# Five modulation vectors summed along the row on VectorE, with the weights' columns on the partitions

## The chip, the cores and the metric

One core of one Trainium2 chip. The metric is device microseconds of one execution of the whole program, the median of three runs. Engines are named as the profile names them: PE is TensorE's matrix multiply, PEld its weight load, DVE is VectorE, ACT ScalarE, POOL GpSimd, and SP the engine whose queue issues nearly all loads.

## The reference, cut to what matters

Two blocks of two residual layers each work on 256 tokens of 1024 features. Each layer takes three vectors of 1024 numbers (shift, scale, gate) from a condition vector `c`:

```
sc = jax.nn.silu(c)
shift, scale, gate = jnp.split(sc @ mod_w[l] + mod_b[l], 3, axis=-1)
hx = modulate(rmsnorm(x, norm_g[l]), shift[:, None], scale[:, None])
...
x = x + gate[:, None] * out_x
```

Block 2 does the same with its own condition `c_2`, six vectors from one weight of 1024 by 6144. Where a second sequence (a context) is modulated too, the same weight is also multiplied by a second condition. The large matrix products between are what most of the time goes to.

## The kernel before, in words

Features lie on the 128 partitions, eight tiles of them, and tokens along the free dimension. Weights come from memory in pieces of 1 MB (128 partitions by 2048), all into one pool of ten slots (`w_p`). A main weight piece is split into a high and a low part (`split`, lines 308 to 310: a cast on ACT at L309 and a subtraction on DVE at L310, in stretches of 512), and every product runs as three products of the parts (`mm3`, L357 to L359).

The modulation weights come through the same pool, 40 chunks of 1 MB after the first eight (`mod_groups`, loads at L502), placed by hand between the main pieces: the lists `L0`, `L1`, `L2`, `L2B` and `L3` give the order of the work in layer 0, layer 1, the mixers of block 2, their output products and the feed-forward, and `md` or `ml` in them means the next chunk. A framework then orders the instructions of each engine by priority, which follows the program's order unless something is put ahead of it, and adds the waits. An instruction with nothing to wait for can be issued far ahead of its place.

Vectors that the context needs too (and three others) are made on TensorE (L515). Five vectors, named in `ON_DVE` at line 85 (`gate1`, `gate2`, `shift3`, `scale3`, `gate3`), are needed for x alone and are made by `x_vector` (lines 468 to 486). A chunk holds two tiles of 128 input features on the partitions, with the 1024 output columns along the row. DVE multiplies each row by its feature's condition value and adds it to a running `part` of 128 by 1024: L476 for the first tile, L478 for the seven others. What is then left is the sum over the 128 partitions, and eight products of `part` with a column of ones on TensorE do that (L482), into a PSUM bank, from which DVE adds the bias (L484). `part` sits in one of the eleven slots of the pool `t4` from the first chunk to the last.

Places that the text speaks of: the end of layer 0, where the steps `ga` and `ra` of `L0` finish and three chunks of `gate1` lie; `residual` (L617 on), which adds the gated output to `X` (L625); and the products begun on an X that is not normed yet (`cols_early`, L606) while the norm is still being computed.

Of the kernel before, what the change touches and what calls it, by code (L numbers as in the profile page):

```python
# [37 lines left out]
# Layer 0 after its first four pieces: weight pieces in order, with modulation chunks (md) between them; the  # L38
# convolution fills what they leave.
# [15 lines left out]
# Layer 1 likewise: (step, group, half).  # L55
# [7 lines left out]
# The mixers of block 2 likewise.  # L63
# [11 lines left out]
# The feed-forward: pairs of up projections, each pair's down projection one piece later.  # L75
# [11 lines left out]
P = 128  # L87
# [48 lines left out]
def pack(inp):  # L136
# [56 lines left out]
    for name, m in L3:  # L193
        if name == "up":
            wp.append(piece_k8(up[:, 128 * m:128 * (m + 1)], up[:, F + 128 * m:F + 128 * (m + 1)]))
        elif name == "down":
# [6 lines left out]
                      for k in range(8)]).reshape(8, KT, P, 256).transpose(0, 2, 1, 3)  # L203
# [3 lines left out]
    mp = np.concatenate([first.reshape(8, P, 2048), full(blk(m0, 2), blk(m1, 0)), half(blk(m1, 1)), half(blk(m1, 2)),  # L207
                         *(half(blk(mw2, i)) for i in range(6))])

    # the convolution's taps in fours, [feature of 32, tap of four] by [feature tile, four, group of 32]  # L210
# [9 lines left out]
           "cst": constants()}  # L220
# [3 lines left out]
def build(tc, gates, wp, mp, vec, xT, cT, c2T, tok, cst, out, dbg=None):  # L224
# [60 lines left out]
    def order_after(i, before):  # L285
        """Keeps two instructions of one engine in order."""
        tc.add_manual_dep(i, before.name, mybir.DependencyInfo(mybir.DependencyClass.NoSync, mybir.DependencyReason.DATA),
                          reason="engine order")

    def act(out, in_, func, **kw):  # L290
        """An activation that needs a table set: kept in order with the others that do."""
        i = nc.scalar.activation(out, in_, func, **kw).ins
        if "last" in tables:
            order_after(i, tables["last"])
        tables["last"] = i
        return i

    def table(name):
        """The table set of the activations that follow."""
# [15 lines left out]
    def halves(raw, width):  # L315
        """A weight piece's parts."""
# [27 lines left out]
    def piece(last=False):  # L344
        """The next weight piece; the ones after it are on their way (fewer behind the last of a layer)."""
# [15 lines left out]
    def mm_w(o, w, x, at, start, stop):  # L361
        """o += w[at].T @ x, in float32 (w and x whole) or in three float32r products of their parts."""
# [5 lines left out]
    def mm_cols(o, w, j, h):  # L368
        """o[128 columns, tokens] over all of D."""
# [3 lines left out]
    def cols2(pc, h):  # L373
        """Two column tiles in one bank."""
# [6 lines left out]
    def toks(o, w, h, s):  # L381
        """o[128 tokens, 256 columns] over all of D."""
# [6 lines left out]
    def mm_rows(banks, pc, x, first, last):  # L389
        """Adds two K tiles (x(k): parts) to all of the 1024 output columns."""  # L390
# [13 lines left out]
    def spread(col):  # L404
        """[128 tokens, 2] -> a bank's [128, 256], the same in all partitions."""
# [8 lines left out]
    def rstd_of(ms, n, eps):  # L414
        """(sum / n + eps) ** -0.5 of [128 tokens, 2] sums, spread over the partitions."""
# [15 lines left out]
    def warm(n):  # L431
        """Keeps the tensor engine's clock up while the first weights arrive."""
        for i in range(n):
            nc.tensor.matmul(warm_bank[0][:, 0:P], ones, ones, start=True, stop=True)
# [8 lines left out]
    def mod_part(k):  # L443
        """Shift and scale of layer 0, for 128 features (one mask, both conditions): partial sums by column tile."""
# [23 lines left out]
    def x_vector(block, c, w, part):  # L468
        """One block for x alone: two K tiles' products summed on the vector engine, the partitions' sums at the end."""
        name, s, bias = block  # L470
        if c == 0:
            part = t4("part", (P, D))
        for i in range(2):
            k = 2 * c + i
            if k == 0:
                nc.vector.tensor_scalar(out=part, in0=w[:, 0, :], scalar1=s[:, 0, 0:1], scalar2=None, op0=ALU.mult)  # L476
            else:
                nc.vector.scalar_tensor_tensor(out=part, in0=w[:, i, :], scalar=s[:, k, 0:1], in1=part, op0=ALU.mult, op1=ALU.add)  # L478
        if c == 3:
            pt = ms_bank()  # L480
            for j in range(8):
                nc.tensor.matmul(pt[:, j:j + 1], part[:, 128 * j:128 * (j + 1)], ones[:, 0:1], start=True, stop=True)  # L482
            o = con.tile([P, 8, 1], F32, name=name)
            nc.vector.tensor_tensor(out=o[:, :, 0], in0=pt[:, 0:8], in1=bias, op=ALU.add)  # L484
            md[name] = o
        return part

    def mod_groups():
        """Modulation vectors, a chunk at a time: [feature, column tile, condition] for one or two blocks of 1024 columns."""
        at = 8  # L490
        late = yield
        for blocks in ((("gate0", S, v("mod_b", 16, 8)), ("shift1", S, v("mod_b", 24, 8))), (("scale1", S, v("mod_b", 32, 8)),),
                       (("gate1", S, v("mod_b", 40, 8)),), (("shift2", S2, v("b_mod_2", 0, 8)),),
                       (("scale2", S2, v("b_mod_2", 8, 8)),), (("gate2", S2, v("b_mod_2", 16, 8)),),
                       (("shift3", S2, v("b_mod_2", 24, 8)),), (("scale3", S2, v("b_mod_2", 32, 8)),),
                       (("gate3", S2, v("b_mod_2", 40, 8)),)):
# [3 lines left out]
            for c in range(chunks):  # L500
# [5 lines left out]
                if blocks[0][0] in ON_DVE:  # L506
                    pm = x_vector(blocks[0], c, w.rearrange("p (k m) -> p k m", k=2), pm)
# [66 lines left out]
    def token_sums(sums):  # L574
        """The sums over a tile's features, [128 tokens, 2]."""
# [5 lines left out]
    def sumsq_all(xs):  # L581
        """Sums of squares of eight feature tiles, in two tiles of four."""
# [10 lines left out]
    def shift_columns(h, sh):  # L593
        """The shift, as two more columns of the scaled X's parts."""
# [4 lines left out]
    def cols_early(pc, h, rs):  # L599
        """Column tiles from X scaled but not yet normed: [(products over the norm, their shift)]."""  # L600
# [16 lines left out]
    def residual(acc, gate, rhs=None, hold=(), early=None, wide=False):  # L617
        """X += gate * acc, and the sums of squares of the new X (wide: by token, in all partitions); hold: products that
        only keep the tensor engine's clock up; early: scale of X and the parts of the scaled X."""
# [38 lines left out]
    # ------------------------------------------------------------ layer 0  # L658
    with ExitStack() as st0:
# [61 lines left out]
        def half_piece(s, g, low):  # L721
            """The high or the low part of half of a piece."""
# [52 lines left out]
        # sigmoid(x) = (1 + tanh(x / 2)) / 2: half of the gates' biases and of the taps that follow one  # L775
# [3 lines left out]
        # 4 * softplus(-lam)  # L779
# [21 lines left out]
        # lower bounds of the forget gates: f = lb + om * (1 + tanh) = lbm + om * tanh  # L801
# [13 lines left out]
        # conv branch  # L815
# [9 lines left out]
        def parts(src):  # L825
            """Two feature tiles as the down projection takes them."""
# [4 lines left out]
        def glu(m, a, g):  # L831
            """Gated input of the convolution for one feature tile, and its taps, which give way to other work."""
# [6 lines left out]
        def shift(m):  # L839
            """[feature of 32, tap of four] on the partitions: a product has four taps."""  # L840
# [6 lines left out]
        def conv(m):  # L847
            """The convolution of one feature tile: its last taps on the tensor engine, the first on the vector engine."""
# [37 lines left out]
        # recurrent branch  # L886
        lru = {}

        def lru_in(m):
            """Projection, short convolution, gates and decay factors of two heads."""  # L890
# [57 lines left out]
        def lru_out(m):  # L948
            """Scans and output gate of two heads; returns the gated output's parts."""
# [6 lines left out]
            for q in range(2):  # L956
                rt, it, tt = lru[m][q]
                nc.vector.tensor_tensor(out=it, in0=it, in1=tt, op=ALU.mult)
                # the context's tokens, then x's; both backwards for the second direction
# [5 lines left out]
            lru[m] = parts(sb)  # L965

        def conv_norm():
            """Layernorm statistics of the conv branch."""
# [548 lines left out]
```

## Time and profile before

| | before |
|---|---|
| median of three runs | 958.51 us (958.29 to 958.64) |
| profiled execution: span | 954.3 us, so 4.2 us lie outside it |
| PE busy | 921.4 us, 97% |
| PEld busy | 863.0 us, 90% |
| DVE busy | 661.0 us, 69% |
| ACT busy | 514.6 us, 54% |
| POOL busy | 16.7 us, 2% |
| DMA | 189.11 MB, mean 198 GB/s |
| mean granted TensorE clock | 0.984 |

A matmul's time on the page runs from its start to its modelled end, and the next one starts before that end. So what a matmul takes of PE is read from start to start, in the order of time, and not from its own length. [...]

### The profile page before, as it was taken

The page shows a single profiled execution, that of the slowest core. Times are in us where ns is not written, and L with a number is a line of the kernel's source. Part 1 is how long each engine was busy: PE and PEld are TensorE (multiplying, and loading weights), DVE is VectorE, ACT ScalarE, POOL GpSimd, SP SyncE. Part 2 cuts the span into 40 slices and gives each one's busy share as a digit, 9 for nine tenths or more (in the row PEclk, how much of TensorE's full clock was granted, in tenths as well). Part 3 has the DMA queues.
Part 4 walks back from the last instruction along what each step waited for, and adds up shares of the span by engine and source line. Part 5 has one row for each costly group of instructions (what it writes and reads, how often), then busy time and mean ns, then how long its engine had stood idle before and what let it go on. Part 6 is the DMA issues. An engine that isn't in the chain of part 4 may idle for free. (4 is left out here: it accounts for less than half of the span.)

```text
span 954.3 us, 18243 instructions
## 1 busy us (share of the span) xinstructions
PE 921.4 (97%) x7638; PEld 863.0 (90%) x7638; DVE 661.0 (69%) x1202; ACT 514.6 (54%) x929; POOL 16.7 (2%) x30
## 2 busy tenths in 40 slices
PE   8999999899978999999999999999999999999996
PEld 7876888696878789999999999899999999999996
DVE  4688787795786775878857344989578866555543
ACT  3454869677554454446543335872564663544442
POOL 0000000000000000000000000000000000000000
PEclk9999999999998899999989999999999999999999
DMA  9968573344665685564643363344746367555511
GB/s 367 408 205 308 177 251 112 116 177 177 225 222 211 234 298 183 208 230 178 256 153 136 136 220 139 140 158 178 264 147 251 133 220 255 188 180 181 194 65 45
DMA packets 31890, 189.11 MB, mean 198 GB/s; under 512 B 3552, under 2 KB 8032, under 8 KB 10688
## 3 DMA queue, kind: packets, MB, share of 16 engines
q1 hardware_dynamic: 31248, 185.46, 53.6%
q0 software_dynamic: 560, 2.49, 0.7%
q8 instruction: 60, 0.98, 0.4%
q14 instruction: 22, 0.18, 0.1%
HBM read 182.23 MB, written 1.05 MB: 192 GB/s over the span
## 5 line engine op out<-in xcount | busy, mean ns | idle before, releaser
L310 DVE TENSOR_TENSOR w<-w 128x512 fp32r<-128x512 f32 x460 | 297.8, 686 | 142.5 <-ACT w L309 97.3
L309 ACT CAST w<-w 128x512 fp32r<-128x512 f32 x460 | 255.5, 617 | 155.0 <-DVE w L310 103.8
L359 PE MATMUL mm<-h4h,w 128*128 128x256 f32 x336 | 94.7, 282 | 0.1
L358 PE MATMUL mm<-h4l,w 128*128 128x256 f32 x336 | 94.3, 281 | 0.0
L357 PE MATMUL mm<-h4h,w 128*128 128x256 f32 x336 | 94.2, 281 | 0.0
L358 PE MATMUL mm<-h2l,w 128*128 128x256 f32 x288 | 81.8, 285 | 0.0
L357 PE MATMUL mm<-h2h,w 128*128 128x256 f32 x288 | 81.6, 284 | 0.0
L359 PE MATMUL mm<-h2h,w 128*128 128x256 f32 x288 | 81.5, 284 | 0.0
L359 PE MATMUL mm<-hxh,w 128*128 128x256 f32 x256 | 73.1, 286 | 4.7 <-DVE w L310 4.7
L357 PE MATMUL mm<-hxh,w 128*128 128x256 f32 x256 | 72.7, 284 | 1.2 <-ACT w L309 1.2
L358 PE MATMUL mm<-hxl,w 128*128 128x256 f32 x256 | 72.2, 282 | 0.0
L359 PE MATMUL mm<-h1h,w 128*128 128x256 f32 x240 | 67.8, 283 | 0.0
L357 PE MATMUL mm<-h1h,w 128*128 128x256 f32 x240 | 67.7, 282 | 0.0
L358 PE MATMUL mm<-h1l,w 128*128 128x256 f32 x240 | 67.7, 282 | 0.0
L359 PEld LDWEIGHTS mm<-h4h,w 128*128 128x128 f32 x336 | 63.5, 189 | 0.3 <-DVE w L310 0.3
L358 PEld LDWEIGHTS mm<-h4l,w 128*128 128x128 f32 x336 | 63.4, 189 | 0.0
L357 PEld LDWEIGHTS mm<-h4h,w 128*128 128x128 f32 x336 | 63.2, 188 | 0.0
L358 PEld LDWEIGHTS mm<-h2l,w 128*128 128x128 f32 x288 | 54.3, 189 | 0.3 <-issue 0.2
L359 PEld LDWEIGHTS mm<-h2h,w 128*128 128x128 f32 x288 | 54.3, 189 | 0.2 <-issue 0.2
L357 PEld LDWEIGHTS mm<-h2h,w 128*128 128x128 f32 x288 | 54.3, 188 | 0.3
L357 PEld LDWEIGHTS mm<-hxh,w 128*128 128x128 f32 x256 | 48.2, 188 | 6.9 <-issue 3.8
L359 PEld LDWEIGHTS mm<-hxh,w 128*128 128x128 f32 x256 | 48.4, 189 | 6.6 <-DVE w L310 6.1
(398 smaller groups left out, 2513.0 us busy)
## 6 DMA issues: line engine op xcount, KB each, us to landing
w<-in_wp SPq DMA_DIRECT2D x115, 1024.0 KB, 4.9
w<-in_mp SPq DMA_DIRECT2D x48, 1024.0 KB, 5.4
four<-up SPq DMA_DIRECT2D x32, 142.0 KB, 3.9
w<-in_wp SPq DMA_DIRECT2D x8, 512.0 KB, 10.7
gw<-in_gates SPq DMA_DIRECT2D x4, 512.0 KB, 3.6
X<-in_xT SPq DMA_DIRECT2D x1, 1024.0 KB, 5.3
ct<-in_cT SPq DMA_DIRECT2D x2, 512.0 KB, 9.3
c<-in_c2T POOLq DMA_DIRECT2D x2, 512.0 KB, 6.3
```

The lines of the kernel that those rows point to most:

```text
L309: a = nc.scalar.copy(hi, src).ins
L310: return a, nc.vector.tensor_tensor(out=lo, in0=src, in1=hi.bitcast(F32), op=ALU.subtract).ins
L357: nc.tensor.matmul(o, wh, xh, start=start, stop=False)
L358: nc.tensor.matmul(o, wh, xl, start=False, stop=False)
L359: nc.tensor.matmul(o, wl, xh, start=False, stop=stop)
```

## The change

The weights of the five vectors are packed transposed. Their columns now lie on the partitions, and the 1024 input features along the row. The condition, as a row of 1024, is loaded into all 128 partitions (`crows`, two of 4 KB a partition, one for each block) and put through Silu on ACT, right after the first `gb` step of layer 0. `x_vector` then multiplies a weight tile by that row on DVE and lets the same instruction sum along the row (`accum_out`), which gives 128 entries of the vector, complete. The product itself is written over the weight tile. The running `part`, the eight products with ones and their PSUM bank are gone; the bias is added in place after the last chunk. The area set aside for loads that POOL issues is made smaller, and the rest of the diff takes comments out.

```
+    mp = np.concatenate([first.reshape(8, P, 2048), full(blk(m0, 2), blk(m1, 0)), half(blk(m1, 1)), half(blk(m1, 2).T),
+                         *(half(blk(mw2, i) if i < 2 else blk(mw2, i).T) for i in range(6))])
...
+           "cst": constants(), "crow": np.stack([np.asarray(inp[n]).reshape(D) for n in ("c", "c_2")])}
...
-    def x_vector(block, c, w, part):
+    def x_vector(block, c, w):
         name, s, bias = block
         if c == 0:
-            part = t4("part", (P, D))
+            md[name] = con.tile([P, 8, 1], F32, name=name)
+        o = md[name]
         for i in range(2):
-            k = 2 * c + i
-            if k == 0:
-                nc.vector.tensor_scalar(out=part, in0=w[:, 0, :], scalar1=s[:, 0, 0:1], scalar2=None, op0=ALU.mult)
-            else:
-                nc.vector.scalar_tensor_tensor(out=part, in0=w[:, i, :], scalar=s[:, k, 0:1], in1=part, op0=ALU.mult, op1=ALU.add)
+            nc.vector.scalar_tensor_tensor(out=w[:, i, :], in0=w[:, i, :], scalar=1.0, in1=s, op0=ALU.mult, op1=ALU.mult,
+                                           accum_out=o[:, 2 * c + i, :])
         if c == 3:
-            pt = ms_bank()
-            for j in range(8):
-                nc.tensor.matmul(pt[:, j:j + 1], part[:, 128 * j:128 * (j + 1)], ones[:, 0:1], start=True, stop=True)
-            o = con.tile([P, 8, 1], F32, name=name)
-            nc.vector.tensor_tensor(out=o[:, :, 0], in0=pt[:, 0:8], in1=bias, op=ALU.add)
-            md[name] = o
-        return part
+            nc.vector.tensor_tensor(out=o[:, :, 0], in0=o[:, :, 0], in1=bias, op=ALU.add)
+
+    crows = [con.tile([P, D], F32, name=f"crow{i}") for i in range(2)]
+
+    def cond_rows():
+        for i, r in enumerate(crows):
+            c = crow[i:i + 1, :]
+            nc.sync.dma_start(r, bass.AP(c.tensor, c.offset, [[0, P], [1, D]]))
+            act(r, r, AF.Silu)
...
-                       (("gate1", S, v("mod_b", 40, 8)),), (("shift2", S2, v("b_mod_2", 0, 8)),),
+                       (("gate1", crows[0], v("mod_b", 40, 8)),), (("shift2", S2, v("b_mod_2", 0, 8)),),
...
             lru[m] = parts(sb)
+            if m == 0:
+                cond_rows()
...
-    nc = bacc.Bacc("TRN2", target_bir_lowering=False, num_devices=1)
+    nc = bacc.Bacc("TRN2", target_bir_lowering=False, num_devices=1, dynamic_dma_scratch_size=2048)
```

## Rows read from the trace of the kernel before

**Rows 1.** The page, busy time and share of each engine.

```profile
PE 921.4 (97%) x7638; PEld 863.0 (90%) x7638; DVE 661.0 (69%) x1202; ACT 514.6 (54%) x929; POOL 16.7 (2%) x30
```

**Rows 2.** Busy time in stretches of 25 us, columns in the first line.

```profile
core 0: us, PE busy (x) PEld busy (x) DVE busy (x) ACT busy (x) POOL busy (x), PEclk, DMA share, GB/s
25.00:50.00 25.00, 23.62 (x216) 19.71 (x213) 15.55 (x34) 10.41 (x20) 0.00 (x0) 1.00 1.00 403
...
250.00:275.00 25.00, 20.83 (x163) 18.64 (x162) 19.25 (x31) 12.08 (x23) 0.00 (x0) 1.00 0.77 292
...
300.00:325.00 25.00, 23.97 (x174) 23.23 (x177) 18.54 (x43) 12.14 (x29) 0.86 (x1) 0.86 0.71 288
...
600.00:625.00 25.00, 23.95 (x198) 22.98 (x197) 24.61 (x40) 22.43 (x35) 0.55 (x1) 1.00 0.36 127
...
800.00:825.00 25.00, 25.00 (x214) 25.00 (x213) 15.00 (x27) 11.40 (x23) 0.00 (x0) 1.00 0.61 213
```

**Rows 3.** The instructions of line 482: durations in ns, first and last start.

```profile
L482 PE MATMUL ms<-ones,part x80: 164/250/353, 315.5 to 817.4; 128*128 128x1 f32 x80
```

**Rows 4.** PE in order of time around the last block (start us, us, what).

```profile
815.60 0.28 PE L359 MATMUL mm<-h4h,w 128*128 128x256 f32 x1
815.71 1.62 PE L482 MATMUL ms<-ones,part 128*128 128x1 f32 x14
817.19 0.36 PE L357 MATMUL mm<-h4h,w 128*128 128x256 f32 x1
817.39 0.28 PE L482 MATMUL ms<-ones,part 128*128 128x1 f32 x2
817.53 0.36 PE L358 MATMUL mm<-h4l,w 128*128 128x256 f32 x1
```

**Rows 5.** PE in order of time at the end of layer 0.

```profile
314.99 0.68 PE L411 MATMUL ms<-dg,ones 128*128 128x128 f32 x4 [0.66 <-DVE dg L407]
315.51 3.14 PE L482 MATMUL ms<-ones,part 128*128 128x1 f32 x16
318.51 0.78 PE L606 MATMUL acc<-e1h,w 128*128 128x258 f32 x2
```

**Rows 6.** Waits from 318 to 325 us (total, times, longest).

```profile
DVE h1l L564 <- ACT h1h L563: 1.8, 1, 1.8
ACT w L309 <- PE acc L606: 1.8, 1, 1.8
```

**Rows 7.** DVE's instructions by line and form (count, busy us, mean ns, idle before).

```profile
L478 DVE SCALAR_TENSOR_TENSOR part<-w,S,part 128x1024 f32<-128x1024 f32 x35 | 44.8, 1281 | 12.7 <-DMA w<-in_mp 12.3
L945 DVE SCALAR_TENSOR_TENSOR tt<-asq,tt 128x1024 f32<-128x1024 f32 x8 | 9.8, 1221 | 14.4 <-ACT asq L944 14.4
...
L476 DVE TENSOR_SCALAR part<-w,S 128x1024 f32<-128x1024 f32 x5 | 3.8, 751 | 3.7 <-DMA w<-in_mp 3.7
...
L1384 DVE TENSOR_SCALAR rv<-bm 128x1 f32<-128x1 f32 x2 | 0.3, 152 | 0.0
```

**Rows 8.** What PE waited for from 225 to 330 us.

```profile
PE mm L359 <- DVE w L310: 4.7, 6, 1.7
```

**Rows 9.** DVE in order of time, ahead of layer 0's residual.

```profile
302.85 2.60 DVE L478 SCALAR_TENSOR_TENSOR part<-w,S,part 128x1024 f32<-128x1024 f32 x2 [1.78 <-DMA w<-in_mp]
305.37 0.87 DVE L625 SCALAR_TENSOR_TENSOR X<-acc,gate,X 128x256 f32<-128x256 f32 x2
```

**Rows 10.** ACT: one group by form, then two instructions in order of time.

```profile
L292 ACT ACTIVATE tt<-tt 128x1024 f32<-128x1024 f32 x8 | 8.1, 1052 | 0.0
...
126.53 0.60 ACT L292 ACTIVATE sb<-mm 128x512 f32<-128x512 f32 x1
...
131.89 0.62 ACT L309 CAST yh<-sb 128x512 fp32r<-128x512 f32 x1 [3.07 <-DVE sb L964]
```

**Rows 11.** Loads: the page's landing time, SP's waits up to 60 us, and line 1154.

```profile
gw<-in_gates SPq DMA_DIRECT2D x4, 512.0 KB, 3.6
...
SPq L692 <- PE ms L448: 11.7, 4, 4.1
...
L1154 DVE MEMSET fg<- x1: 72/72/72, 1.0 to 1.0; 128x16 f32 x1
```

More of the change, by code (lines that the diff above doesn't have):

```diff
@@ L206, in pack @@
     blk = lambda w, i: w[:, D * i:D * (i + 1)]
-    mp = np.concatenate([first.reshape(8, P, 2048), full(blk(m0, 2), blk(m1, 0)), half(blk(m1, 1)), half(blk(m1, 2)),
-                         *(half(blk(mw2, i)) for i in range(6))])
+    mp = np.concatenate([first.reshape(8, P, 2048), full(blk(m0, 2), blk(m1, 0)), half(blk(m1, 1)), half(blk(m1, 2).T),
+                         *(half(blk(mw2, i) if i < 2 else blk(mw2, i).T) for i in range(6))])
     taps = np.concatenate([inp["ev_conv_w"][0], np.zeros((1, D), np.float32)]).reshape(8, 4, 8, 4, 32)
@@ L219, in pack, with build @@
     arr = {"gates": gates, "wp": wp, "mp": mp, "vec": vec, "xT": act[0], "cT": act[1], "c2T": act[2], "tok": tok,
-           "cst": constants()}
+           "cst": constants(), "crow": np.stack([np.asarray(inp[n]).reshape(D) for n in ("c", "c_2")])}
     return {k: np.ascontiguousarray(v) for k, v in arr.items()}
-def build(tc, gates, wp, mp, vec, xT, cT, c2T, tok, cst, out, dbg=None):
+def build(tc, gates, wp, mp, vec, xT, cT, c2T, tok, cst, crow, out, dbg=None):
     nc = tc.nc
@@ L492, in mod_groups @@
         for blocks in ((("gate0", S, v("mod_b", 16, 8)), ("shift1", S, v("mod_b", 24, 8))), (("scale1", S, v("mod_b", 32, 8)),),
-                       (("gate1", S, v("mod_b", 40, 8)),), (("shift2", S2, v("b_mod_2", 0, 8)),),
-                       (("scale2", S2, v("b_mod_2", 8, 8)),), (("gate2", S2, v("b_mod_2", 16, 8)),),
-                       (("shift3", S2, v("b_mod_2", 24, 8)),), (("scale3", S2, v("b_mod_2", 32, 8)),),
-                       (("gate3", S2, v("b_mod_2", 40, 8)),)):
+                       (("gate1", crows[0], v("mod_b", 40, 8)),), (("shift2", S2, v("b_mod_2", 0, 8)),),
+                       (("scale2", S2, v("b_mod_2", 8, 8)),), (("gate2", crows[1], v("b_mod_2", 16, 8)),),
+                       (("shift3", crows[1], v("b_mod_2", 24, 8)),), (("scale3", crows[1], v("b_mod_2", 32, 8)),),
+                       (("gate3", crows[1], v("b_mod_2", 40, 8)),)):
             nb = len(blocks)
@@ L506, in mod_groups @@
                 if blocks[0][0] in ON_DVE:
-                    pm = x_vector(blocks[0], c, w.rearrange("p (k m) -> p k m", k=2), pm)
+                    x_vector(blocks[0], c, w.rearrange("p (k m) -> p k m", k=2))
                     tc.cur_priority = here
```

## The prediction

> **What bounds the kernel now.** First the busy shares: PE 97%, DVE 69%, ACT 54% [rows 1]. A busy PE alone proves little, because matmul ends are modelled, so next come the stretches of 25 us [rows 2]. The reader is to see three kinds. From about 325 us on nearly every stretch looks like 800 to 825: PE 25.00 of 25, DVE 15.00. There PE issues without a hole, and what it no longer has to issue comes off the end. At 600 to 625 DVE is at 24.61 and PE at 23.95: DVE decides now and then. At 250 to 275 PE has 20.83; there PE waits for other engines, and the waits name DVE's subtraction L310 (4.7 us in six waits) [rows 8]. So the same microsecond on DVE is free in the first kind, half paid in the second and fully paid in the third. The three runs have a median of 958.5 us; the sum is made against the profiled span of 954.3 us, and 4.2 us outside it stay as they are.
>
> **What goes: the eight products with ones, five times.** They are 80 entries on PE, each of one column [rows 3], 16 for a vector. What they take is read from start to start. Around the last block [rows 4], 815.60 to 817.53 is 1.93 us and holds, beside the block, one L359 and one L357 of 0.11 us each (815.60 to 815.71); the block is worth 1.93 - 0.22 = 1.7 us. Three more blocks (starts at 552, 647 and 687 us) look alike, in stretches that PE fills. Four times 1.7 is 6.8 us. I take all of it; the low end is 5.1 us, with one block lost where DVE decides.
>
> The fifth block, of `gate1`, is another thing. It stands at the end of layer 0, 315.51 to 318.51 us, 3.0 us for the same 16 entries [rows 5], in a stretch with a mean granted clock of 0.86 [rows 2]; PE had just stood idle 0.66 us for DVE's dg and been through short products [rows 5]. PE isn't what is last there: X has to be normed on DVE and ACT first. But behind the block come the early products L606, and ACT's next cast waits 1.8 us for them; being in order it holds the h1h behind it, and DVE's h1l waits 1.8 us for that [rows 6]. So the block sits in the chain through ACT. Without it the cast starts 1.8 us earlier, and the next late thing is DVE's own work on h1l. I take 1.8 us; ends 0 (another chain is as late) and 3.0 (all of it).
>
> **What comes: the sum along the row on DVE.** Each vector had one L476 (0.751 us) and seven L478 (1.281 us). It now has eight products of two SBUF operands with an immediate scalar, written over an operand. That is exactly the form of L945: 1.221 us [rows 7]. No row shows the accumulator's output. From below its price is 0 (the instruction reads and writes the same elements as L945); a gain beyond that I exclude, since nothing is taken out of it. From above it is one more small instruction with its gap; the nearest row is a 128x1 operation of 0.152 us [rows 7], and I put 0.25 us as the upper end, for lost overlap. I take the row, 0.15, so 1.37 us each.
>
> [...]
>
> Where it is paid:
> - Six of `gate1`'s eight run between 258 and 270 us, where PE waits for DVE [rows 8]: before 0.751 + 5 x 1.281 = 7.16 us, after 6 x 1.37 = 8.23, so +1.1 us on the path (ends +0.2 and +1.7).
> - The last two run right ahead of layer 0's residual, 302.85 to 305.37 us [rows 9]: 2.60 before, 2.74 after, +0.1 (ends -0.2 and +0.3).
> - In the mixers five run between 603 and 648 us, four L478 and one L476: 4 x 0.09 + 0.62 = 1.0 us more on a DVE that is nearly full; half of it on the path, +0.5 (ends 0 and +1.5).
> - The other 27 lie where PE is full and DVE idle for 10 us of 25 [rows 2]: 0. If that cover went, 27 x 0.15 = 4 us.
> The bias addition L484 stays but no longer waits for PE. Sum of the new work: +1.7 us, ends 0 and 3.5.
>
> **What is new beside it.** Two Silu over 128x1024 on ACT: L292 of that size takes 1.05 us, so 2.1 us. They are chained behind the Silu of the first `gb` step (126.53 us), and behind that ACT stands idle 3.07 us for DVE's sb before the cast at 131.89 [rows 10]. That hole hides them: 0. The table of functions is the one just used. If the loads were late, casts and the convolution's copies queued behind them on ACT would wait, and PE behind those; without the cover it is 2.1 us.
>
> Two loads of 512 KB on SP. A load of that size lands in 3.6 us [rows 11], and nothing in its tile has to come free first. Such an instruction may be issued long before its place: L1154's memset, which belongs to layer 1, ran at 1.0 us [rows 11]. If the loads are pulled into the first 50 us, where the DMA is full at 403 GB/s [rows 2], 1.05 MB are 2.6 us. But the main loads there are paced by slots, not by memory: SP waits 11.7 us for PE's L448 [rows 11], so a queue that falls behind can catch up. I take 0, upper end 2.6. SP is moved past nothing else: chunks, sizes and their slots are as before, and the slot is freed by the same DVE instruction, as it was. On POOL only the area for its own loads shrinks; POOL is busy 2% [rows 1], 0. `part`'s slot in `t4` and five PSUM banks come free, for which no wait in the rows stands: 0.
>
> **The sum.** -6.8 - 1.8 + 1.7 = -6.9 us: a span of 947.4 and a time of 951.6 us. With all good ends, -6.8 - 3.0 + 0 = -9.8, 948.7 us; with all bad ends, -5.1 + 3.5 + 2.1 + 2.6 = +3.1, 961.6 us.
>
> **Rivals.**
> 1. The accumulator makes the instruction twice as long, 2.44 us. For it: no row shows an accumulator at all. Against it: with two SBUF operands L945 takes no more than 1.221 us [rows 7], so both reads fit in one pass. Its place is the end of layer 0: 6 x 2.44 - 7.16 = +7.5, the pair ahead of the residual 4.88 - 2.60 = +2.3, half of 4 x 1.16 + 1.69 in the mixers = +3.2. With -8.6 from PE that is +4.4, 962.9 us: slower. Some ten and a half instructions are on the path, so it decides from about 0.8 us more for each. [...]
> 2. What PE saves in the mixers is given back. For it: DVE 24.61 of 25 at 600 to 625 [rows 2]. Then the blocks at 647 and 687 us and `gate1`'s bring nothing, two blocks remain: -3.4 + 1.7 = -1.7, 956.8 us, no difference. Against it: the two blocks stand in issue order between main products without a wait before them, as in [rows 4].
> 3. More comes back at layer 0's end. The block runs at a lower granted clock (0.86 as a mean of its 25 us, and 3.0 us for what takes 1.7 elsewhere) [rows 2, 4, 5]; with other products in its place the clock may be up sooner and all 3.0 us come, with a cheap accumulator: 948.9 us. For it: PE's hole of 0.66 us and the short products stand right ahead of the block [rows 5]. Against it: DVE is next in line.
> 4. The framework orders anew, because instructions have other lengths, and the hand-made order suffers somewhere by more than 10 us, some 961 us.
> That the products stay is no rival: nothing in the diff calls them.
>
> **How the numbers follow.** Forecast 0.58, rival 1 0.11, rival 2 0.13, rival 3 0.14, rival 4 0.04. A measurement can tell 0.2%, some 1.9 us, from no change. Faster by more than that: forecast and rival 3, 0.72. Within it: rival 2, 0.13. Slower: rivals 1 and 4, 0.15. The range leaves out rivals 1 and 4 and a little more at both ends: 947.0 to 959.0 us.
>
> **What would show it.** Right: no L482; PE's 16 entries gone without a hole in their place; the new DVE instruction at 1.2 to 1.5 us with its read; the half-rate stretch near 316 us shorter; ACT's Silu between 127 and 132 us with no wait for its load. Wrong: DVE products over 2 us; longer waits of PE for L310 between 258 and 275 us; more holes of PE between 600 and 690 us; the loads of the rows among the first ten; later starts of the first main products near 15 us.

## The result, and the profile after

| | before | after |
|---|---|---|
| median of the first comparison | 958.40 us (956.51 to 958.64, 4 runs) | 947.34 us (939.29 to 951.13, 4 runs) |
| profiled execution: span, time, clock | 954.3 us, -, 0.984 | 947.3 us, 949.14 us, 0.979 |
| PE busy, instructions | 921.4 us, 7638 | 916.0 us, 7558 |
| DVE busy | 661.0 us | 658.9 us |
| ACT busy | 514.6 us | 516.9 us |

The ratio is 0.9883, with a 95% interval of 0.9836 to 0.9931: about 11 us faster. Two more comparisons of the same two kernels gave 0.9884 (0.9854 to 0.9913) and 0.9886 (0.9844 to 0.9929). Single executions of one kernel lie up to 12 us apart, and the long ones have a lower mean granted clock (after: 939.29 us at 0.994, 951.13 us at 0.977), which matters for everything below.

The busy shares of after, which answer [rows 1]:

```profile
PE 916.0 (97%) x7558; PEld 857.4 (91%) x7558; DVE 658.9 (70%) x1242; ACT 516.9 (55%) x931; POOL 16.4 (2%) x30
```

PE lost the 80 entries. DVE has 40 more, and they are reads of the accumulator; its busy time is even a little less. The groups of DVE's instructions by form in after (count, busy us, mean ns, idle before), answering [rows 7]:

```profile
L476 DVE SCALAR_TENSOR_TENSOR w<-w,crow 128x1024 f32<-128x1024 f32 x40 | 47.6, 1219 | 15.8 <-DMA w<-in_mp 15.8
L476 DVE DVE_READ_ACCUMULATOR w<-w,crow 128x1 f32 x40 | 3.2, 81 | 0.0
```

The product takes 1.219 us, the time of L945 before, and its read 0.081 us. DVE of after in order of time, among `gate1`'s products at the end of layer 0:

```profile
259.10 1.22 DVE L476 SCALAR_TENSOR_TENSOR w<-w,crow 128x1024 f32<-128x1024 f32 x1
260.24 0.08 DVE L476 DVE_READ_ACCUMULATOR w<-w,crow 128x1 f32 x1
260.24 1.22 DVE L476 SCALAR_TENSOR_TENSOR w<-w,crow 128x1024 f32<-128x1024 f32 x1
261.39 0.08 DVE L476 DVE_READ_ACCUMULATOR w<-w,crow 128x1 f32 x1
```

From 259.10 to 260.24 is 1.14 us from one product to the next, and the next starts at the same instant as the read. So the accumulator's read costs no time of DVE's queue here. An L478 of before takes 1.20 us on the same count:

```profile
259.73 1.28 DVE L478 SCALAR_TENSOR_TENSOR part<-w,S,part 128x1024 f32<-128x1024 f32 x1
260.93 1.29 DVE L310 TENSOR_TENSOR w<-w 128x512 fp32r<-128x512 f32 x2
```

What PE waited for from 225 to 330 us in after (us in total, times, longest), answering [rows 8]:

```profile
PE mm L359 <- DVE w L310: 4.8, 5, 1.7
```

Stretches of 25 us of after, to lay beside [rows 2] (same columns):

```profile
250.00:275.00 25.00, 21.00 (x155) 19.12 (x154) 17.73 (x34) 10.53 (x21) 0.00 (x0) 0.91 0.77 274
300.00:325.00 25.00, 24.23 (x191) 20.05 (x191) 18.59 (x44) 10.25 (x24) 0.86 (x1) 0.93 0.81 313
600.00:625.00 25.00, 22.76 (x185) 21.58 (x184) 23.77 (x46) 21.26 (x31) 0.55 (x1) 0.99 0.35 125
800.00:825.00 25.00, 25.00 (x212) 25.00 (x211) 16.50 (x33) 11.40 (x23) 0.00 (x0) 1.00 0.66 227
```

The stretch at 800 is as full as it was, only its products come earlier. At 300 the clock is up from 0.86 to 0.93 and PE has 191 products instead of 174. At 250 and at 600 the clock is lower than before (0.91 and 0.99, where it was 1.00).

ACT of after in order of time, answering [rows 10], with the idle time before an instruction in brackets:

```profile
126.88 2.00 ACT L292 ACTIVATE crow<-crow 128x1024 f32<-128x1024 f32 x2
128.78 0.60 ACT L309 CAST w<-w 128x512 fp32r<-128x512 f32 x1
129.28 0.47 ACT L863 ACTIVATE cv<-acc,V 128x256 f32<-128x256 f32 x1
132.68 0.62 ACT L309 CAST yh<-sb 128x512 fp32r<-128x512 f32 x1 [2.93 <-DVE sb L966]
```

Both Silu run where the prediction put them, without a wait, and ACT stands idle for DVE's `sb` behind them as before (2.93 us, before 3.07). The last ACT_TABLE_LOAD ahead of them, 1.28 us, starts at 125.09 us, before the Silu of the `gb` step at 126.39; none stands between that Silu and these two. The group of the row loads on the page of after (count, KB, us to landing), answering [rows 11]:

```profile
crow<-in_crow SPq DMA_DIRECT2D x2, 512.0 KB, 8.6
```

The loads were issued at 44.1 and 45.7 us, in the stretch with the DMA full (a share of 1.00 and 401 GB/s from 25 to 50 us), and took 8.6 us to land, not 3.6 us.

To compare places, the trace of each kernel was cut at the same products. These are the lengths of five stretches in us, each worked out from the starts of two products in the order of time. "Gate1's sums" runs from the last product on the context's parts (`mm<-hch`) to layer 0's last (`acc<-yh`), "end of layer 0" from there to the first `mm<-dh`, "552" from the first to the last `mm<-w,h2ch`, "mixers" from the first `ms<-vc` to the first `mm<-oah`, "816" from the first to the last `mm<-h4h`.

| kernel profiled | gate1's sums | end of layer 0 | 552 | mixers | 816 |
|---|---|---|---|---|---|
| before | 91.83 | 53.91 | 18.52 | 102.63 | 173.80 |
| before, small area | 91.76 | 53.99 | 18.51 | 102.63 | 173.80 |
| before without gate1's products | 92.21 | 48.32 | 18.51 | 102.64 | 173.78 |
| before without any of the products | 91.66 | 49.96 | 16.77 | 98.87 | 172.00 |
| after | 95.20 | 50.11 | 16.77 | 101.31 | 171.98 |
| after, second profile | 91.96 | 50.07 | 16.77 | 101.08 | 172.02 |
| after, third profile | 91.98 | 48.43 | 16.78 | 100.16 | 172.01 |
| after with the products put back | 92.69 | 53.38 | 18.51 | 105.93 | 173.78 |

A half-rate stretch is one whose granted clock is 0.50 in the trace, as in before from 315.80 to 322.60 us; outside such stretches it is 1.00. Products with a weight tile and 256 columns (`mm<-h2ch`) follow each other by 0.21 us in the one of before at 496 us, and by 0.12 us (`mm<-h2h`, `mm<-h2ch`) at 507 us, behind it. Outside the five stretches of the table the kernels differ by half-rate stretches that come and go between executions of one kernel. One between 488 and 503 us, 10.2 us long, stands in the profile of before and in two of the three of after, and is worth 3.5 us (53.4 against 49.9 us from the first `mm<-h2ch` to the first `mm<-w,h2ch`).

### The profile page after: what moved, and what is told of

Same layout as the page of the kernel before. It is cut to its first block, busy times and chain, and to the rows that moved or that the text cites. A ratio compares the mean times of both kernels' runs of the same rounds, so it can differ in the third digit from the quotient of the medians.

```text
span 947.3 us, 18121 instructions
## 1 busy us (share of the span) xinstructions
PE 916.0 (97%) x7558; PEld 857.4 (91%) x7558; DVE 658.9 (70%) x1242; ACT 516.9 (55%) x931; POOL 16.4 (2%) x30
## 4 chain that ended last, share of the span: by engine, by line
PE 37%; issue 11%; DVE 4%; ACT 1%; POOL 0%; POOLq 0%; DVEq 0%
PE mm L359 8%; PE mm L358 8%; PE mm L357 8%; PE acc L357 3%; PE acc L359 3%; PE acc L358 3%; PE mm L385 1%; PE mm L387 1%; PE mm L386 1%; DVE w L476 0%; DVE lx L1267 0%; PE ms L645 0%; ACT L292 0%; DVE xa L564 0%; PE ms L1295 0%
## 5 line engine op out<-in xcount | busy, mean ns | idle before, releaser
L310 DVE TENSOR_TENSOR w<-w 128x512 fp32r<-128x512 f32 x460 | 297.0, 684 | 140.7 <-ACT w L309 94.5
L359 PE MATMUL mm<-hxh,w 128*128 128x256 f32 x256 | 74.2, 290 | 4.8 <-DVE w L310 4.8
L357 PE MATMUL mm<-hxh,w 128*128 128x256 f32 x256 | 74.1, 289 | 1.2 <-ACT w L309 1.2
L476 DVE SCALAR_TENSOR_TENSOR w<-w,crow 128x1024 f32<-128x1024 f32 x40 | 47.6, 1219 | 15.8 <-DMA w<-in_mp 15.8
L357 PEld LDWEIGHTS mm<-hxh,w 128*128 128x128 f32 x256 | 49.4, 193 | 7.3 <-issue 5.0
L359 PEld LDWEIGHTS mm<-hxh,w 128*128 128x128 f32 x256 | 49.4, 193 | 6.5 <-DVE w L310 6.0
L357 PEld LDWEIGHTS mm<-h2h,w 128*128 128x128 f32 x288 | 54.6, 189 | 0.4 <-PE ms L1367 0.2
```

The costliest lines, as they stand in the source:

```text
L310: return a, nc.vector.tensor_tensor(out=lo, in0=src, in1=hi.bitcast(F32), op=ALU.subtract).ins
L357: nc.tensor.matmul(o, wh, xh, start=start, stop=False)
L359: nc.tensor.matmul(o, wl, xh, start=False, stop=stop)
L476: nc.vector.scalar_tensor_tensor(out=w[:, i, :], in0=w[:, i, :], scalar=1.0, in1=s, op0=ALU.mult, op1=ALU.mult, accum_out=o[:, 2 * c + i, :])
```

## The experiments

For medians that the clock disturbs, one more number is worked out: a least-squares line through the 159 executions here whose clock is on record, with one slope and a level for each kernel. The slope is 0.63 us of span for each 0.001 of mean granted clock, and the executions scatter about it by 0.8 us. The level at a clock of 0.985 is called "at equal clock". Most of what a change gains by raising the clock is taken out by this, so both numbers are needed. The levels have errors of 0.1 us (before) to 0.4 us (four executions).

| kernel | runs | median us | median clock | span at equal clock | against before |
|---|---|---|---|---|---|
| before | 66 | 954.8 to 955.5 by comparison | 0.984 | 952.8 | |
| after (three comparisons) | 16 | 947.34, 944.62, 941.79 | 0.982, 0.986, 0.991 | 943.7, 944.1, 943.4 | -9.1, -8.6, -9.4 |
| before, small area | 12 | 953.49 | 0.986 | 952.5 | -0.3 |
| before without any of the products | 5 | 941.55 | 0.991 | 942.4 | -10.4 |
| before without gate1's products | 12 | 948.67 | 0.990 | 949.2 | -3.6 |
| after with the products put back | 12 | 957.42 | 0.982 | 953.7 | +0.9 |
| after with each DVE product twice | 6 | 960.77 | 0.978 | 955.3 | +2.5 |
| after without the condition's rows | 4 | 946.46 | 0.984 | 943.8 | -8.9 |
| after, three chunks at layer 1's start | 4 | 947.52 | 0.983 | 944.6 | -8.2 |
| after, three chunks spread in layer 1 | 10 | 951.90 | 0.978 | 946.8 | -6.0 |
| after, one chunk later (two comparisons) | 12 | 943.08, 942.27 | 0.988, 0.990 | 943.1, 942.8 | -9.7, -10.0 |

### After again

> The changed kernel once more, unaltered, to see how its times spread. Theory 1 (the products on TensorE paid for the gain): median 945 to 950 us, span 1.8 us below the time in every run. Theory 2 (the half-rate stretches of the clock, which fall differently from run to run, make much of the difference): spans scatter over 10 us or more and go with the mean granted clock, about 6 to 7 us for 0.010 of clock, and the kernel before scatters in the same way.

944.62 us, ratio 0.9884 (0.9854 to 0.9913). Time and span of one execution stand 1.8 us apart, and before's do so by 1.9 to 2.0 us in these runs (952.09 and 950.2 us, say). The 4.2 us "outside the span" of the prediction were the span of one execution and the median of others.

### The smaller area for POOL's loads

```
-    nc = bacc.Bacc("TRN2", target_bir_lowering=False, num_devices=1)
+    nc = bacc.Bacc("TRN2", target_bir_lowering=False, num_devices=1, dynamic_dma_scratch_size=2048)
```

> The kernel before with one edit: the area for POOL's own loads at 2048 bytes. Theory 1 (the area costs nothing): 958.5 us and 4.2 us outside the span, as before. Theory 3 (the area is what takes 2.4 us outside the span): span as before, some 954 us, 1.8 us outside it, time 956.1 us.

953.49 us, ratio 0.9984 (0.9963 to 1.0004), and 1.9 to 2.0 us outside the span. It does nothing that these runs can tell; the theory that the area shortens what lies outside the span has fallen.

### Before without the products

```
-            pt = ms_bank()
-            for j in range(8):
-                nc.tensor.matmul(pt[:, j:j + 1], part[:, 128 * j:128 * (j + 1)], ones[:, 0:1], start=True, stop=True)
...
-            nc.vector.tensor_tensor(out=o[:, :, 0], in0=pt[:, 0:8], in1=bias, op=ALU.add)
+            nc.vector.tensor_tensor(out=o[:, :, 0], in0=part[:, 0:8], in1=bias, op=ALU.add)
```

> The kernel before without the 40 products with ones: the running part's first eight columns take the place of the sums, so the five vectors aren't the reference's. DVE's work stays. Theory 1: the products are worth 6.8 us in four places and 1.8 us at the end of layer 0, so 958.5 - 8.6 = 949.9 us, 4.2 us outside the span. Rival 2 of the prediction (given back in the mixers): 955 us or more.

941.55 us, ratio 0.9851 (0.9826 to 0.9877), for a kernel that leaves out the sum over the partitions. That is 14 us, and 10.4 us at equal clock, where 8.6 us stood in the sum. In the table of stretches the three places of the four later blocks give 1.75, 3.76 (two blocks) and 1.80 us, in sum 7.3 us against 6.8 us predicted. What is left over sits at the end of layer 0: 53.91 to 49.96 us.

### The products put back into after

```
+            pt = ms_bank()
+            for j in range(8):
+                nc.tensor.matmul(pt[:, j:j + 1], w[:, 1, 128 * j:128 * (j + 1)], ones[:, 0:1], start=True, stop=True)
+            nc.vector.scalar_tensor_tensor(out=o[:, :, 0], in0=pt[:, 0:8], scalar=0.0, in1=o[:, :, 0], op0=ALU.mult, op1=ALU.add)
```

> The changed kernel with eight products of a weight tile with ones put back for each vector; their result is multiplied by 0 and added, so that they count for time only. Theory 1: the time goes up by 6.8 us (four places) to 9.8 us (with 3.0 us at the end of layer 0), to about 954 to 957 us. If the products were not what paid, it stays at 947.

957.42 us, ratio 1.0018 (1.0003 to 1.0034): all of the gain goes, 12.8 us against the 944.62 us of the same comparison. So the 80 entries on PE are what the change lives on. The stretches return to those of before, the end of layer 0 to 53.38 us. Only the mixers overshoot, 105.93 against 102.63 us; a half-rate stretch of 6.8 us lies in them that before doesn't have (a mean granted clock of 0.86 from 625 to 650 us, where before has 1.00).

### Before without gate1's products alone

```
-            pt = ms_bank()
-            for j in range(8):
-                nc.tensor.matmul(pt[:, j:j + 1], part[:, 128 * j:128 * (j + 1)], ones[:, 0:1], start=True, stop=True)
+            pt = part
+            if name != "gate1":
+                pt = ms_bank()
+                for j in range(8):
+                    nc.tensor.matmul(pt[:, j:j + 1], part[:, 128 * j:128 * (j + 1)], ones[:, 0:1], start=True, stop=True)
```

> The kernel before without the eight products with ones (16 entries on PE) of gate1 alone; the other four vectors keep theirs, and gate1 is left uncomplete. Theory A (prediction): the block at the end of layer 0 is worth 1.8 us: some 953.6 against 955.4. Theory B (rival 3 of the prediction): the whole block with its half-rate part comes, 3.0 us or more: 952.4 or less. Theory C, what the traces without products suggest (some 4 us between the end of layer 0 and 363 us, 1.7 of it a shorter half-rate stretch): 951 to 951.6.

948.67 us, ratio 0.9941 (0.9916 to 0.9965), where before has 955.28 us: 6.6 us from one block that was priced at 1.8 us. At equal clock it is 3.6 us; the other 3 us are a higher clock, 0.990 against 0.984. Theory A has fallen, theory B's 3.0 us is passed by far, and theory C's 4 us is what is there at equal clock, but not the whole.

The profiles say how. PE in order of time at the end of layer 0, without the block; the rows to lay beside are [rows 5]:

```profile
314.82 0.68 PE L411 MATMUL ms<-dg,ones 128*128 128x128 f32 x4 [0.66 <-DVE dg L407]
315.44 3.64 PE L517 MATMUL ms<-w,S 128*32 128x512 f32 x32
319.01 1.24 PE L608 MATMUL acc<-e1h,w 128*128 128x258 f32 x8
320.08 0.95 PE L525 MATMUL ms<-C,row 128*128 128x4 f32 x8
320.89 0.60 PE L608 MATMUL acc<-e1h,w 128*128 128x258 f32 x3
321.33 1.84 PE L608 MATMUL acc<-e1l,w 128*128 128x258 f32 x14
323.01 0.28 PE L357 MATMUL mm<-h1h,w 128*128 128x256 f32 x1
```

Where the 16 entries of one column stood, 32 products of the next modulation chunks stand (L515 before, L517 here). Counted from layer 0's last product (309.12 us here, 309.29 us before) the first product on the normed X comes 13.9 us behind it and had come 14.1 us behind it, hardly sooner. But the 32 are then done. Before has them behind; PE by those products' line alone, in the two parts of the end of layer 0, first before (L515), then without the block (L517), columns PE, PEld, granted clock, DMA share, GB/s:

```profile
309.30:323.40 14.10, 0.00 (x0) 0.00 (x0) 0.76 0.61 259
323.40:363.20 39.80, 7.90 (x64) 1.57 (x64) 1.00 0.73 264
```

```profile
309.10:323.00 13.90, 3.64 (x32) 0.94 (x32) 1.00 0.84 337
323.00:357.40 34.40, 4.26 (x32) 0.63 (x32) 1.00 0.77 275
```

Before has none of the 64 in the first part and all in the second; without the block it is 32 and 32, and the second part is 5.4 us shorter. The mean clock of the first part goes from 0.76 to 1.00: the half-rate stretch of 6.8 us, from 315.8 us on (0.50), isn't there. The rows of before behind the block show what it does: 11 early products in 2.5 us, where eight take 1.07 us in the kernel without the block. They also show PE's only later hole, 0.37 us:

```profile
318.51 2.71 PE L606 MATMUL acc<-e1h,w 128*128 128x258 f32 x11
321.02 2.56 PE L606 MATMUL acc<-e1l,w 128*128 128x258 f32 x14
324.19 0.51 PE L606 MATMUL acc<-e1l,w 128*128 128x258 f32 x2 [0.37 <-DVE e1l L649]
```

So PE is full around the block, but for holes of 0.66 and 0.37 us, and the length of the end of layer 0 can be taken apart: PE's holes (gaps over 0.02 us), half the length of the half-rate stretch in it, an estimate (a stretch of 3.4 us makes after's second profile longer than its third by 1.64 us, 50.07 against 48.43), and the rest, which is PE's own work at the full rate.

| kernel profiled | end of layer 0 | holes | lost to half rate | rest |
|---|---|---|---|---|
| before | 53.91 | 1.03 | 3.41 | 49.47 |
| before, small area | 53.99 | 1.10 | 3.41 | 49.47 |
| before without gate1's products | 48.32 | 0.66 | 0 | 47.66 |
| before without any of the products | 49.96 | 0.66 | 1.71 | 47.60 |
| after | 50.11 | 0.77 | 1.71 | 47.63 |
| after, third profile | 48.43 | 0.77 | 0 | 47.65 |
| after with the products put back | 53.38 | 0.77 | 3.41 | 49.19 |

With the block the rest is 49.2 to 49.5 us, without it 47.6 to 47.7 us. Of the 5.6 us that the place gains here, 1.8 us are the block's own time at the full rate, 3.4 us the half-rate stretch and 0.4 us the hole. The 32 products stand in this stretch in both kernels; moved up, they keep PE full and add nothing to that sum. By the line above a half-rate stretch of 6.8 us counts for only 2.3 us (0.0036 of mean clock), so some 1.1 us of it is left in the 3.6 us at equal clock. What brings the higher clock, the block's going or the 32 products in its place, this edit doesn't tell, as it changes both.

The same two rows of after with the products put back show the old picture again, 0 and 64 and a clock of 0.76:

```profile
311.90:326.10 14.20, 0.00 (x0) 0.00 (x0) 0.76 0.68 257
326.10:365.30 39.20, 7.90 (x64) 1.57 (x64) 1.00 0.75 269
```

### After with each DVE product twice

```
+            nc.vector.scalar_tensor_tensor(out=w[:, i, :], in0=w[:, i, :], scalar=1.0, in1=s, op0=ALU.mult, op1=ALU.mult)
```

> The changed kernel with each of its 40 DVE products done twice (the second without the sum, over a weight tile that nobody reads again): 40 instructions of 1.14 us more on DVE, nothing else. Theory A, the prediction's own accounting of where DVE decides (six at 250 to 275 us, two ahead of layer 0's residual, half of five in the mixers, 10.5 on the path): 10.5 x 1.14 = +12 us over the changed kernel's 944.6, so some 956.6. Theory B, DVE has room nearly everywhere and PE catches up behind it (the changed kernel's trace gave back only about 0.4 us at 217 to 284 us): under +4 us, below 948.6. Theory C, DVE decides in more places than that: over +18 us, above 962.

960.77 us, ratio 1.0061 (1.0040 to 1.0083). Against after it is 11.6 us at equal clock (955.3 less 943.7), and 13 to 19 us by the medians (after's three are 947.34, 944.62 and 941.79 us), with a clock of 0.978. Theory A has the sum at equal clock, but not its places. Against the third profile of after, gate1's sums grow by 7.3 us (99.33 less 91.98), where eight times 1.14 is 9.1; the mixers grow by 11.1 us (111.23 less 100.16), where 2.9 was expected. There one wait does it, PE's longest from 640 to 680 us (us in total, times, longest):

```profile
PE acc L1313 <- DVE st L1324: 6.5, 1, 6.5
```

The 25 us around it, with the columns of [rows 2]:

```profile
650.00:675.00 25.00, 18.50 (x145) 17.80 (x143) 24.54 (x43) 4.41 (x8) 0.86 (x1) 0.90 0.48 174
```

DVE is at 24.54 of 25 there: a queue that is full, with a step in it that PE waits for. A half-rate stretch of 10.2 us, from 670 us on, follows that hole and makes part of the 11.1 us; with another of 3.4 us at 625 us the clock takes up to 6.8 us of them. "816", where PE was full, grows too, by 1.8 us (173.77 less 172.01), so the cover isn't complete there once DVE has this much more to do. The duplicate also measures the accumulator by itself; DVE's instructions by form in this kernel, first the second copy without the sum, then the first with it:

```profile
L478 DVE SCALAR_TENSOR_TENSOR w<-w,crow 128x1024 f32<-128x1024 f32 x40 | 47.9, 1220 | 0.0
L476 DVE SCALAR_TENSOR_TENSOR w<-w,crow 128x1024 f32<-128x1024 f32 x40 | 47.6, 1221 | 14.7 <-DMA w<-in_mp 14.7
```

1220 ns without, 1221 ns with it.

### After without the condition's rows

```
-            c = crow[i:i + 1, :]
-            nc.sync.dma_start(r, bass.AP(c.tensor, c.offset, [[0, P], [1, D]]))
-            act(r, r, AF.Silu)
+            nc.gpsimd.memset(r, 1.0)
```

> The changed kernel without the two 512 KB loads of the condition rows and without their two Silu; the rows are filled with ones on POOL instead, so the five vectors lose their condition. Theory A (prediction): loads and Silu are hidden, 0 +- 1 us against the changed kernel's 944.6. Theory B: the loads, which the trace shows at 44 to 46 us in a stretch with the DMA full, cost their 2.6 us: 942.0. Theory C: the Silu cost too, 2.1 us more: 939.9.

946.46 us (4 runs, 941.16 to 948.35), and 943.8 us at equal clock against 943.7 of after. The two loads and the two Silu cost nothing that these four runs can tell (the level's error is 0.4 us); theories B and C are out at equal clock.

### Gate1's chunks later, three and one

Three chunks moved to layer 1's start, or spread there; one chunk moved:

```
-MB = (6, 0)
+MB = (9, 0)
...
-    ('ml', 1), ('ml', 1), ('ml', 1), ('rb', 3), ('ml', 1), ('ga', 2), ('ra', 0), ('ga', 3), ('ra', 2), ('ra', 1),
+    ('ml', 1), ('rb', 3), ('ga', 2), ('ra', 0), ('ga', 3), ('ra', 2), ('ra', 1),
```

> The changed kernel with the three chunks of gate1 that stood in layer 0's list moved to layer 1's start, so that six DVE products (6 x 1.14 = 6.8 us) leave the end of layer 0. Theory A: DVE decides there, and PE is full where they go: 3 to 6 us less than 944.6, so 939 to 942. Theory B: nine chunks in a row take the queue ahead of layer 1's own weights; 9 MB at 403 GB/s are 23 us of loads, PE waits for weights behind them: slower than 947. Theory C: DVE at the end of layer 0 isn't on the path: 944 to 946.

947.52 us, 8.2 us below before at equal clock, no better than after. Gate1's sums are short, 87.74 us, 4.2 us less than in after; the end of layer 0 takes 57.69 us, 9.3 us more than in the third profile of after (3.4 us of it through a half-rate stretch of 6.8 us from 326 us on, 4.9 us through more holes of PE). Nine chunks of 1 MB are in the queue from 300 to 330 us, and the DMA share at 300 to 325 is 0.97. But PE's longest hole there is for a piece's low part, which DVE makes:

```profile
326.41 0.58 PE L359 MATMUL mm<-h1h,w 128*128 128x256 f32 x1 [2.35 <-DVE w L310]
```

And DVE is late with it because it has the moved products to do first. Five of them run back to back from 319.46 to 325.19 us, while ACT had begun to cast that piece at 322.51 us, so it had landed. The last of the five, and the subtraction:

```profile
324.04 1.22 DVE L476 SCALAR_TENSOR_TENSOR w<-w,crow 128x1024 f32<-128x1024 f32 x1
325.68 0.68 DVE L310 TENSOR_TENSOR w<-w 128x512 fp32r<-128x512 f32 x1
```

So what DVE gives at one place it takes at the next; that the loads cost anything besides isn't shown.

> As the kernel with gate1's three chunks moved to layer 1's start, but the three are spread between layer 1's own pieces, so that no run of nine chunks stands ahead of layer 1's weights. Theory A: 3 to 6 us less than the changed kernel's 944.6 (939 to 942), and at least as good as the kernel with the nine in a row. Theory B (the queue's order is what matters): better than that kernel by over 2 us. Theory C: DVE at the end of layer 0 isn't on the path: 944 to 946.

951.90 us, ratio 0.9952 (0.9929 to 0.9975), 3 us worse than after at equal clock: theory B fell, the spread is the worse of the two. PE's wait for L310 at the same place is 5.1 us, with the same five products of DVE ahead of it (321.34 to 327.07 us), and the stretch behind the end of layer 0 is longer too (134.19 us from the first `mm<-dh` to the first `mm<-h2ch`, 129.78 in after).

> The changed kernel with only the last of gate1's three layer-0 chunks moved to layer 1's start (two DVE products, 2.3 us). The kernel with all three moved had gained 3 us by 309 us and lost it again by 363 us. Theory A: two products fewer ahead of layer 0's residual and only one chunk more in layer 1's queue bring 1 to 2 us: 942.5 to 943.5 against 944.6. Theory B: what is gained at layer 0's end is lost at layer 1's start here too: 944 to 946.

> The changed kernel again, beside the kernel with one chunk of gate1 later, in one call. Expected 944.6 us as before, +- 1.5, ratio 0.988. It is the base for the other.

> The kernel with one chunk of gate1 later again, now beside the changed kernel. Theory A: it is 1 to 1.5 us faster than the changed kernel of the same call (943.1 against 944.6 in separate calls, and 0.7 to 1.0 us at an equal mean clock). Theory B: the two don't differ, under 0.7 us in the medians; the difference of the separate calls was the clock of their executions.

With only the last of the three moved (six chunks at layer 1's start become seven) the medians are 943.08 and 942.27 us, after's beside the second 941.79 us. By the medians they don't differ; at equal clock the one-chunk kernel is lower by 0.8 us (943.0 against 943.7, each with an error of some 0.2). That is too near the bound to call it faster than after. Both beat before by 1.1 to 1.3%.

## Why the prediction came out as it did

The forecast was 951.6 us, in a range of 947.0 to 959.0; 947.34 us came, at the range's low end, and 944.62 and 941.79 us in the later comparisons, below it. The sign was right, and so was the main mechanism, the 80 entries gone from PE. One step of it and some sizes were off, in this order:

- **The block of gate1**, priced at 1.8 us. It is worth 3.6 us at equal clock and 6.6 us by the medians. The step that failed is "PE isn't what is last there", and with it the chain through ACT from which the price was read. The chain did get shorter: ACT's wait of 1.8 us isn't among those of after from 318 to 328 us. But the first product on the normed X came only 0.2 us sooner, counted from layer 0's last product, and of the chain no more than the hole of 0.4 us for `e1l` came back. PE has no other hole behind the one for `dg`, so the block pays with its own time on PE, 1.8 us at the full rate; that the wait read from ACT has the same size is luck. What the sum left out is the half-rate stretch over the block and the products behind it, 3.4 us. Together that is 5.6 us at this place, and the two profiles without a half-rate stretch there make it 5.6 and 5.5 us (53.91 to 48.32 and 48.43). Rival 3 named the clock; its 3.0 us was too little, as it counted the half rate over the block alone.
- **The four later blocks**: 1.75 + 3.76 + 1.80 = 7.3 us in the stretches, 6.8 us as the difference of the two experiments without products at equal clock (10.4 less 3.6). The term was 6.8 us. Right, and [rows 4] is where it was read.
- **The DVE's new work**, +1.7 us. The prediction took durations where the queue is paid from start to start. No run shows the 0.15 us that it put on for the accumulator: the read takes 0.081 us and starts together with the next product. Each new instruction is 1.14 us from start to start instead of 1.37 us, an old L478 1.20 us instead of 1.281 us. So only the five that take the place of an L476 are longer. At gate1's sums +0.1 us is left of +1.2 (91.98 against 91.83 us); PE's wait for L310 stayed as it was, as its row of after shows next to [rows 8]. In the mixers it is +1.3 us (100.16 less 98.87) for +0.5, inside its ends. The lengths of the five make +0.1 us of it; PE's holes there are 1.1 us longer (2.84 against 1.78 us). The order of DVE changed there: the steps on `gv` run ahead of the state's update. PE's wait for that update is 0.7 us in both, though; what is new are a wait of 0.6 us for DVE's `lx` and 0.5 us more for ACT's `wt`. That the order brings them isn't shown. At equal clock after lies 1.3 us above the kernel without products (943.7 less 942.4), so the sum of the term holds within the errors, and its places are swapped. That the sum comes near is luck.
- **The clock.** The first profile of after has two more half-rate stretches at gate1's sums than the others, 3.4 and 6.8 us long, and that place is 95.20 us; the two later profiles and the one without the rows have 91.9 to 92.0 us. So the 6.9 us of the profiled spans, just what was forecast, are a chance: more was gained at the end of layer 0, and 3.2 us were lost to the clock.
- **What lies outside the span**: 4.2 us were carried over; 1.8 us is what after has. With it the same sum gives 949.2 us.
- **The nulls**: loads, Silu, the area, each 0, each borne out by an experiment or by the profile. The loads were issued at 44 us, as feared in the bound. That is behind the first main products (15.06 us against 15.29 us before), so these say nothing of them; the run without the rows does: the level at equal clock is the same.

**Rival 1** is refuted by one row: 1219 ns for two SBUF sources of 128 by 1024 in f32 with an accumulator, 1220 ns for the same without one. The rival's 2.44 us was twice L945's 1.221 us, and no run shows it. What the rival would have cost was weighed about right: DVE's products done twice are 5.5 us above before in the same comparison (960.77 against 955.31 us), where its sum had 4.4 us.

**Rival 2**, the mixers give it back, holds for a third: 1.3 of 3.8 us without a half-rate stretch, and up to 2.4 us with one (101.31 less 98.87). **Rival 4**, a new order that hurts by 10 us, didn't come, but its small form did, in the mixers.

What stays open is the half-rate stretch in the mixers, between 619 and 636 us. It stands in the profiles of eight of the ten runs of kernels that sum along the row on DVE, and in none of the four of kernels that don't: from 625 to 650 us the mean granted clock is 0.94 in after, 0.86 with the products put back and 0.93 with DVE's products done twice, and 1.00 in before, with the small area and without any of the products. At 3.4 us of length it costs some 0.9 us (101.08 against 100.16). The changed order of DVE there is the likely reason; it wasn't tried by itself, as the order at that place follows from when its inputs are ready. Open too is why the end of layer 0 keeps its clock without the block (1.00 from 309.1 to 323.0 us).

## What to carry to other kernels

Before a removed piece is priced by the chain that it seems to sit in, see whether the engine itself has holes around it. Where it had next to none here (0.66 and 0.37 us), the piece was worth its start-to-start time at a granted clock of 1.00 (1.8 us), whatever chain ran beside it, and 32 products that stood behind moved up into its place. Then read the granted clock over the piece and what follows: a half-rate stretch there is a term of its own in the sum, here 3.4 us, and it needs a range from 0 up. Take a stretch of the trace apart into holes, clock and rest, and compare the rests. Work moved away from a queue that is late at one place must find room in the same queue elsewhere: moving gate1's chunks only moved DVE's delay (gate1's sums 4.2 us shorter, the end of layer 0 9.3 us longer). And set the base of a sum from one execution: its own span and its own time, never a span from one and a median from others.

## What the runs showed of the hardware that was not expected

- The sum along the row in the same DVE instruction is free in these kernels: 1221 ns with it and 1220 without, and the next product starts at the same instant as the read of 0.081 us. The read is an instruction of its own in the trace, DVE_READ_ACCUMULATOR, 40 of them at 81 ns.
- A fixed program differs by over 1% between executions on one chip: after took 938.95 to 950.40 us in its third comparison. The time goes with the mean granted clock, 0.63 us for each 0.001. Half-rate stretches of 3.4, 6.8 or 10.2 us appear at a handful of places: from 175.8, 288.4, 315.8 and 493.2 us on in before, from 249.1, 273.0, 290.1, 317.4, 491.5 and 624.6 us on in after, one from 326 us on with three chunks at layer 1's start, and one from 670 us on with DVE's products done twice. At the end of the program the clock is low too (0.51 from 942.0 us on in after), with PE idle. Which of them appear changes from one execution to the next: over 300 to 325 us after has 0.93 in its first profile and 1.00 in its third.
- The half-rate stretch at 312 to 325 us is 6.8 us long in all three profiles of kernels with gate1's block there: the mean granted clock is 0.76 over 14.1 us in before, 0.76 over 14.2 us with the products put back, and 0.86 from 300 to 325 us with the small area. Where the block is gone and the chunks stand as they did it is 3.4 us or none. After has 3.4, 3.4 and 0 in its three profiles (an end of layer 0 of 50.11, 50.07 and 48.43 us), the kernel without any of the products 3.4 (0.93 from 300 to 325 us) and the one without gate1's 0 (1.00).
